# Attention part of a hybrid layer: softmax steps given priority, rotated blocks spread over the heads, weight halves moved from GpSimd to VectorE

## The chip, the cores and the metric

The kernel runs on one core of one Trainium2 chip. The metric is the device time of one execution in microseconds (us); lower is better. Times of whole runs are medians over several executions. The profile is one further execution recorded by the hardware profiler. PE is TensorE's matmul side, PEld its weight loads, DVE is VectorE, ACT is ScalarE, POOL is GpSimd, SP is SyncE, which issues most DMAs.

## The reference

One decoder layer on 1040 tokens (16 meta tokens and 1024 of input) of width 1024, in float32. A big projection gives the operands of two parallel branches: a retention with 4 heads and a differential attention with 8 heads. Both are merged by gates, and a gated MLP with a short convolution follows. The change touches the projections and the attention:

```
proj = u_pad @ w_in
rq, rk, rv, rg, dq, dk, dv, gates = split(proj)
rq = rope(rq); rk = rope(rk) * RET_DK ** -0.5
dq = rope(rmsnorm(dq, q_norm_w)); dk = rope(rmsnorm(dk, k_norm_w))
s = einsum('bhcqd,bhckd->bhcqk', dq_block, dk) * scale
p = softmax(where(mask, s, NEG))
a = p[:, :, 0] - lam * p[:, :, 1]
o = einsum('bhqk,bhke->bhqe', a, dv)
```

## The kernel before, in words

Float32 products are made of three fp32r matmuls: every operand is split into a high part and a low part (the rest), and high x high, high x low and low x high are summed in PSUM. For a weight block of 1024 x 128 this split is `split_half` (L226), called twice from `load_w` (L231): ACT casts half a block from `wr` into `wh` (L228), and POOL subtracts it from `wr` to give `wl` (L229), 128 x 512 elements each. `next_w` (L212) keeps two blocks loaded ahead.

`phase1` makes the projections and the 8 attention heads together. `projections` (L609) is a generator that works through a list of 128-column blocks, `seq`; each block is three accumulations of 24 matmuls into the two `acc` banks, and `evacuate` (L532) takes each one out of PSUM. What it costs depends on the kind. An `rv`, `rg`, `gd` or `gr` block costs one DVE multiply for each accumulation (L606). A `dk` or `dq` block costs ACT squares, a shuffle (L570) and multiplies on DVE (L571, L573) and POOL (L572). The rotary blocks `rk` and `rq` come in pairs: the first of a pair is only copied by ACT (L543); at the second, DVE makes two products from PSUM (L550, L551) and two more steps (L554, L555), and POOL makes two steps (L552, L553). L554 overwrites the buffer `x1` that L552 reads, so DVE waits there for POOL.

`attention(h)` (L661) is the other generator: eight blocks of 128 queries. For each block, `scores` makes the two score matrices on PE; DVE adds the mask and takes the row minimum (the scores carry a minus sign) (L686, L692); ACT makes the exponentials with row sums (L693); DVE inverts the sums (L697, L698); ACT scales the second matrix (L699); DVE combines both (L700). Then `turn` (L704) transposes the result on PE (L709), ACT and DVE split it (`ah`, `al`, L241 and L246), and PE multiplies it with the values into `ot`. Two query blocks are turned together, so each head has four groups of turns; in the first the second block has 272 columns, in the others 528, 784 and 1040. `prepare` (L622) splits keys and queries of the next head (L636, L637) and stacks them by DMAs from POOL's queue.

`blend` (L162) interleaves both generators: each attention step carries a weight, and 58 units of the projections, six to a block, are spread over a head. The instructions so recorded are then put in order by the framework's scheduler: each has a priority by its place in the program, and a model of the engines decides at what time which one goes first. Each engine then executes its own list in that order. PE's list follows the program nearly everywhere.

The list `seq` puts between the three blocks of each head's attention (dk, dq, dv) seven others. Before the change those are four `rv` blocks, then all 16 rotary blocks, then the remaining `rv` and `rg` blocks and the gates. So the rotary blocks fall into heads 0 to 2.

Of the kernel before, what the change touches and what calls it, by code (L numbers as in the profile page):

```python
# [13 lines left out]
AF = mybir.ActivationFunctionType  # L14
ALU = mybir.AluOpType
AX = mybir.AxisListType
# [12 lines left out]
RH, DH = 4, 8  # L29
# [68 lines left out]
class Builder:  # L98
    ATT_WEIGHT, RET_WEIGHT = 38.666666666666664, 27.0

    def __init__(self, ctx, tc, a, chunk_dec):
        self.tc, self.nc, self.a = tc, tc.nc, a
        self.chunk_dec = chunk_dec
        nc = self.nc
        self.V, self.A, self.G, self.E, self.S = nc.vector, nc.scalar, nc.gpsimd, nc.tensor, nc.sync
        pool = lambda n, b=1, **k: ctx.enter_context(tc.tile_pool(name=n, bufs=b, **k))
        self.cp = pool("cst")
        self.bp = pool("big", 34)
        self.wp = pool("w", 2)
        self.tp = pool("tmp", 2)  # L110
        self.ps = pool("ps", 2, space=PSUM)
        self.dr = pool("dr", 1, space=DRAM)
        self.n = 0
        self.later = []
        self.rot = 0

# [114 lines left out]
    def load_w(self, blk):  # L231
        w = self.tile_w()
        for i in (0, 4):
            self.split_half(w, self.raw_half(blk, i), i)
        return w

    def split(self, dh, dl, src, eh="A", el="V", scale=None):
# [423 lines left out]
    def attention(self, h):  # L661
        V, A, G, E, S = self.V, self.A, self.G, self.E, self.S
# [7 lines left out]
        def scores(t0, m, n, pieces):  # L670

            sm = self.tmp("sm", n=16, bufs=4)
            s = []
            for c in range(2):
                sc_ = self.big() if m > 2 else self.tmp("hs", n=16)
                for i, (a0, sz) in enumerate(pieces):
                    ps = self.sc()
                    self.mm(ps[:m, :sz], QA[c][:, t0:t0 + m], K[c][:, a0:a0 + sz], True, False)
                    self.mm(ps[:m, :sz], QB[c][:, t0:t0 + m], K[c][:, a0:a0 + sz], False, True)
                    if m == 2:  # L680
                        mk = self.hm[:m, :sz]
                    elif i == len(pieces) - 1:
                        mk = self.mask[:, 584 - sz:584]
                    else:
                        mk = self.mask[:, :sz]
                    V.tensor_tensor_reduce(out=sc_[:m, a0:a0 + sz], in0=ps[:m, :sz], in1=mk, scale=1.0, scalar=3e38,  # L686
                                           op0=ALU.add, op1=ALU.min, accum_out=sm[:m, 4 * c + i:4 * c + i + 1])
                np_ = len(pieces)
                mx = sm[:m, 4 * c:4 * c + 1]
                if np_ > 1:  # L690
                    mx = sm[:m, 4 * c + 3:4 * c + 4]
                    V.tensor_reduce(out=mx, in_=sm[:m, 4 * c:4 * c + np_], axis=AX.X, op=ALU.min)  # L692
                A.activation(sc_[:m, :n], sc_[:m, :n], AF.Exp, bias=mx, scale=-1.0,  # L693
                             accum_out=sm[:m, 10 + c:11 + c])
                s.append(sc_)
                yield 0.2 + n / 1000
            V.reciprocal(sm[:m, 12:14], sm[:m, 10:12])  # L697
            V.tensor_mul(sm[:m, 13:14], sm[:m, 13:14], self.nlam[:m])  # L698
            A.activation(s[1][:m, :n], s[1][:m, :n], AF.Copy, scale=sm[:m, 13:14])  # L699
            V.scalar_tensor_tensor(out=s[0][:m, :n], in0=s[0][:m, :n], scalar=sm[:m, 12:13], in1=s[1][:m, :n],  # L700
                                   op0=ALU.mult, op1=ALU.add)
            return s[0]

        def turn(pieces, meta=None):  # L704
# [18 lines left out]
        def rows(c):  # L723
            n = NMETA + P * (c + 1)
            k = -(-n // 512)
            sz = [2 * (n // (2 * k))] * k
            sz[0] += n - sum(sz)
            return (yield from scores(NMETA + P * c, P, n, [(sum(sz[:i]), sz[i]) for i in range(k)]))
# [3 lines left out]
        self.spill["do", h] = d, db  # L732
        outs = [(14, 258), (272, 256), (528, 256), (784, 256)]
        halo = yield from scores(HALO, 2, NMETA, [(0, NMETA)])
        ahead = yield from rows(0)

# [4 lines left out]
        for b in range(2):  # L741
            ps = self.tr()
# [5 lines left out]
        ps = self.tr()  # L748
# [4 lines left out]
        for p in range(4):  # L753
# [31 lines left out]
            for jj in range(p + 1):  # L785
# [4 lines left out]
                for kk in range(2):  # L790
                    j = 2 * jj + kk
                    lo = 128 if last and kk == 1 else 0
                    out = ot[:, o0 + lo:nq]
# [6 lines left out]
            t0, n = outs[p]  # L800
# [16 lines left out]
    def phase1(self):  # L817
        a = self.a
        self.spill = {}
        off = dict(rq=0, rk=8, rv=16, rg=32, dq=48, dk=56, dv=64, gr=72, gd=80)  # L820
        item = lambda k, i: (k, i, off[k] + i)
        dtiles = lambda h: [item("dk", h), item("dq", h), item("dv", h)]
        fill = []
        for h in range(RH):
            fill += [item("rk", 2 * h), item("rk", 2 * h + 1), item("rq", 2 * h), item("rq", 2 * h + 1)]
        for h in range(RH):
            fill += [item("rv", 4 * h + e) for e in range(4)] + [item("rg", 4 * h + e) for e in range(4)]
        fill = fill[16:20] + fill[:16] + fill[20:]
        fill += [item("gd", i) for i in range(8)] + [item("gr", i) for i in range(8)]
        seq = dtiles(0)  # L830
        for h in range(DH):
            f = fill[7 * h:7 * h + 7]
            dt = dtiles(h + 1) if h + 1 < DH else []
            seq += f[:3] + dt[:2] + f[3:4] + dt[2:] + f[4:]
        seq += fill[7 * DH:]
        order = []
        for n in range(0, NF, 2):
            down = [a["w_down"][n - 2], a["w_down"][n - 1]] if n else []
            up = [a["w_up"][f] for f in (n, NF + n, n + 1, NF + n + 1)]
            order += up[:2] + down + up[2:] if n < NF - 2 else up + down  # L840
        order += [a["w_down"][NF - 2], a["w_down"][NF - 1]]
        self.loaded = []
        self.stream = ([a["w_in"][b] for _, _, b in seq] + [a["w_ret_o"][i] for i in range(16)]
                       + [a["w_diff_o"][i] for i in range(8)] + [a["w_out"][i] for i in range(8)] + order)
        with self.tc.manual_schedule():
            self.norm_in()
            gen = self.projections(seq[2:])
            units = 6 * (len(seq) - 2)
            for _ in range(15):
                next(gen)  # L850
                units -= 1
        for _ in self.prepare(0):
            next(gen)
            units -= 1
        for _ in range(5):
            next(gen)
            units -= 1
        for h in range(DH):
            n = 58
            self.blend(self.attention(h), self.ATT_WEIGHT, gen, n)  # L860
            units -= n
        return gen, units


# [442 lines left out]
```

## Time and profile before

| | |
|---|---|
| median of 3 runs | 2567.45 us (2563.02 to 2570.38) |
| the profiled execution's own time | 2568.86 us |
| its span, first to last instruction | 2567.1 us |
| mean granted clock of TensorE | 0.993 |
| PE busy | 2509.6 us, 98% |
| DVE busy | 1550.9 us, 60% |
| ACT busy | 904.0 us, 35% |
| POOL busy | 816.8 us, 32% |
| the 8 heads, from the first score of head 0 to the end of head 7 | 108.5 to 1239 us of the span |

How to read it: matmuls overlap each other, so a busy PE can still be slower than it might be; what counts is the time in which PE or PEld stood idle, and what ended that wait. A head's window below runs from its first score matmul to that of the next head.

### The profile page before, as it was taken

To read this page: it belongs to the slowest core of one execution; us is meant where nothing else is said; L and a number is where in the kernel's file an instruction comes from. 1 tells how busy PE (TensorE), PEld (TensorE's weight loads), DVE (VectorE), ACT (ScalarE), POOL (GpSimd) and SP (SyncE) were. 2 spreads that over 40 slices of the span, in tenths; PEclk is the share of its full clock that TensorE was granted. 3 is DMA by queue.
4 is the path that set the end of the run, shared out by engine and by line. 5 is a ranking of instruction groups with operands and counts; after the bars stand their busy time and mean duration, and the time that the engine had idled before them with its cause. 6 is when DMAs were issued, how large, how long until landed. Compare 5 with 4: busy or idle time off the path is not lost. (4 is left out here: it accounts for less than half of the span.)

```text
span 2567.1 us, 40420 instructions
## 1 busy us (share of the span) xinstructions
PE 2509.6 (98%) x15444; PEld 2416.9 (94%) x15444; DVE 1550.9 (60%) x3228; ACT 904.0 (35%) x1881; POOL 816.8 (32%) x649
## 2 busy tenths in 40 slices
PE   8999999999999999999999999999999999999999
PEld 8899998999999999999998899999999999999998
DVE  7665757556463737453787887652555566555555
ACT  5343444444343525333466553332311111111111
POOL 1424343322222222222333332434332333333232
PEclk9999999999999999999999999999999999999999
DMA  4524242323324242423443434522111111111112
GB/s 165 129 84 108 63 115 71 107 76 93 104 81 120 62 121 65 117 84 104 116 107 90 105 99 134 185 93 99 38 50 46 50 50 41 50 50 42 50 50 87
DMA packets 171538, 224.55 MB, mean 87 GB/s; under 512 B 26712, under 2 KB 109264, under 8 KB 171344
## 3 DMA queue, kind: packets, MB, share of 16 engines
q1 hardware_dynamic: 165440, 202.70, 26.1%
q0 software_dynamic: 5760, 19.17, 3.5%
q8 instruction: 121, 1.98, 0.3%
q14 instruction: 73, 0.60, 0.1%
q10 hardware_dynamic: 144, 0.10, 0.0%
HBM read 160.20 MB, written 42.35 MB: 79 GB/s over the span
## 5 line engine op out<-in xcount | busy, mean ns | idle before, releaser
L175 PE MATMUL acc<-b,wh 128*128 128x342 f32 (+3 forms) x5948 | 1451.0, 326 | 15.7 <-DVE b L429 9.2
L175 PEld LDWEIGHTS acc<-b,wh 128*128 128x128 f32 x5948 | 1033.7, 190 | 28.4 <-issue 9.2
L175 PE MATMUL acc<-b,wl 128*128 128x342 f32 (+3 forms) x2974 | 966.9, 325 | 1.5 <-POOL wl L229 1.5
L229 POOL TENSOR_TENSOR wl<-wr,wh 128x512 fp32r<-128x512 f32 x366 | 507.6, 1404 | 1148.8 <-ACT wh L228 1136.5
L175 PE MATMUL sc<-b,wh 128*128 128x342 f32 (+2 forms) x2580 | 648.6, 334 | 1.1 <-ACT b L241 1.1
L175 PEld LDWEIGHTS acc<-b,wl 128*128 128x128 f32 x2974 | 564.1, 190 | 7.7 <-POOL wl L229 2.6
L175 PEld LDWEIGHTS sc<-b,wh 128*128 128x128 f32 x2580 | 455.2, 189 | 22.5 <-ACT b L241 1.3
L175 PE MATMUL sc<-b,wl 128*128 128x342 f32 (+2 forms) x1290 | 429.3, 334 | 0.0
L228 ACT CAST wh<-wr 128x512 fp32r<-128x512 f32 x366 | 212.8, 618 | 574.9 <-issue 241.2
L175 PEld LDWEIGHTS sc<-b,wl 128*128 128x128 f32 x1290 | 243.8, 189 | 10.0
L246 POOL TENSOR_TENSOR b<-b,b 128x512 fp32r<-128x512 f32 (+1 forms) x86 | 138.3, 1608 | 304.9 <-ACT b L241 262.7
L606 DVE TENSOR_TENSOR ev<-acc,b 128x342 f32<-128x342 f32 (+1 forms) x144 | 74.0, 514 | 187.7 <-PE acc L175 184.1
L241 ACT CAST b<-b 128x512 fp32r<-128x512 f32 (+3 forms) x137 | 102.1, 750 | 214.0 <-DVE b L1242 145.6
L693 ACT ACTIVATE b<-b,sm 128x272 f32<-128x272 f32 (+7 forms) x128 | 101.0, 789 | 150.4 <-DVE sm L692 118.6
L1205 DVE SCALAR_TENSOR_TENSOR b<-b,cols,b 128x1024 f32<-128x1024 f32 x88 | 148.8, 1691 | 2.3
L686 DVE CUSTOM_DVE_ANT_0 b<-sc,consts 128x144 f32<-128x144 f32 (+6 forms) x224 | 106.6, 503 | 39.3 <-PE sc L175 38.6
L1196 DVE TENSOR_TENSOR b<-sc,b 128x342 f32<-128x342 f32 x84 | 42.5, 511 | 139.4 <-PE sc L175 139.4
L246 DVE TENSOR_TENSOR al<-sc,ah 128x512 fp32r<-128x512 f32 (+2 forms) x144 | 77.6, 539 | 68.3 <-ACT ah L241 68.0
L241 ACT CAST ah<-sc 128x512 fp32r<-128x512 f32 (+2 forms) x144 | 67.3, 467 | 121.8 <-PE sc L709 84.0
L1220 DVE TENSOR_TENSOR b<-b,sc 128x512 f32<-128x512 f32 x117 | 78.7, 683 | 48.8 <-PE sc L175 48.8
L175 PE MATMUL sc<-b,b 128*128 128x264 f32 (+9 forms) x480 | 96.8, 319 | 1.9 <-DVE sm L686 1.9
L1203 DVE TENSOR_SCALAR b<-b,cols 128x1024 f32<-128x1024 f32 x44 | 81.5, 1853 | 1.6
(248 smaller groups left out, 2665.4 us busy)
## 6 DMA issues: line engine op xcount, KB each, us to landing
wr<-w_in SPq DMA_DIRECT2D x170, 256.0 KB
wr<-w_up SPq DMA_DIRECT2D x88, 256.0 KB
d<-ev SPq DMA_DIRECT2D x120, 171.0 KB
b<-b POOLq DMA_DIRECT2D x72, 260.0 KB, 4.6
b<-d SPq DMA_DIRECT2D x256, 64.0 KB
b<-d SPq DMA_DIRECT2D x24, 513.0 KB
wr<-w_down SPq DMA_DIRECT2D x44, 256.0 KB
b<-d SPq DMA_DIRECT2D x32, 260.0 KB
```

Source lines behind the costliest of these rows:

```text
L175: self.E.matmul(out, lhsT=l, rhs=r, start=start, stop=stop)
L228: self.A.copy(h, raw)
L229: (self.G if el == "G" else self.V).tensor_sub(l, raw, h.bitcast(F32))
L241: self.A.copy(dh, src)
L246: (self.V if el == "V" else self.G).tensor_sub(dl, src, dh.bitcast(F32))
L606: V.tensor_mul(o[:, :n], ps[:, :n], self.rb[:, cs])
L686: V.tensor_tensor_reduce(out=sc_[:m, a0:a0 + sz], in0=ps[:m, :sz], in1=mk, scale=1.0, scalar=3e38, op0=ALU.add, op1=ALU.min, accum_out=sm[ ...
L693: A.activation(sc_[:m, :n], sc_[:m, :n], AF.Exp, bias=mx, scale=-1.0, accum_out=sm[:m, 10 + c:11 + c])
L1196: self.V.tensor_mul(up[:, t0:t0 + n], ps[:, :n], self.rb2[:, t0:t0 + n])
L1203: V.tensor_scalar(out=o[:, q], in0=up[:, q], scalar1=self.cw(2, fi), scalar2=self.cb(fi), op0=ALU.mult, op1=ALU.add)
L1205: V.scalar_tensor_tensor(out=o[:, q], in0=up[:, NMETA - 2 + i:T - 2 + i], scalar=self.cw(i, fi), in1=o[:, q], op0=ALU.mult, op1=ALU.add)
L1220: self.V.tensor_add(h, h, ps)
```

## The change

Four edits, all in `phase1` and what it calls.

1. `load_w` takes the engine of the low part from `self.low`. It is "V" (DVE) while the loop over the 8 heads runs and "G" (POOL) otherwise.
2. The softmax instructions on DVE and ACT (L686 to L700 of before) are recorded with `high_priority(offset=300)`: the scheduler treats them as if they stood 300 places earlier.
3. The seven filler blocks of a head become five light ones and one pair of rotary blocks, in place of 16 rotary blocks in a row.
4. The order of the light blocks follows (rv and rg of each retention head, then gd, then gr).

```
+        self.low = "G"
...
-            self.split_half(w, self.raw_half(blk, i), i)
+            self.split_half(w, self.raw_half(blk, i), i, self.low)
...
-                    V.tensor_tensor_reduce(out=sc_[:m, a0:a0 + sz], in0=ps[:m, :sz], in1=mk, scale=1.0, scalar=3e38,
-                                           op0=ALU.add, op1=ALU.min, accum_out=sm[:m, 4 * c + i:4 * c + i + 1])
+                    with self.tc.high_priority(offset=300):
+                        V.tensor_tensor_reduce(out=sc_[:m, a0:a0 + sz], in0=ps[:m, :sz], in1=mk, scale=1.0, scalar=3e38,
+                                               op0=ALU.add, op1=ALU.min, accum_out=sm[:m, 4 * c + i:4 * c + i + 1])
...
+            with self.tc.high_priority(offset=300):
+                V.reciprocal(sm[:m, 12:14], sm[:m, 10:12])
+                V.tensor_mul(sm[:m, 13:14], sm[:m, 13:14], self.nlam[:m])
+                A.activation(s[1][:m, :n], s[1][:m, :n], AF.Copy, scale=sm[:m, 13:14])
+                V.scalar_tensor_tensor(out=s[0][:m, :n], in0=s[0][:m, :n], scalar=sm[:m, 12:13], in1=s[1][:m, :n],
+                                       op0=ALU.mult, op1=ALU.add)
...
+        light = [item(k, 4 * h + e) for h in range(RH) for k in ("rv", "rg") for e in range(4)]
+        light += [item("gd", i) for i in range(8)] + [item("gr", i) for i in range(8)]
+        pairs = [[item(k, 2 * h), item(k, 2 * h + 1)] for h in range(RH) for k in ("rk", "rq")]
         fill = []
...
-        fill = fill[16:20] + fill[:16] + fill[20:]
-        fill += [item("gd", i) for i in range(8)] + [item("gr", i) for i in range(8)]
+        for h in range(DH):
+            fill += light[5 * h:5 * h + 5] + pairs[h]
+        fill += light[5 * DH:]
...
+        self.low = "V"
         for h in range(DH):
             n = 58
             self.blend(self.attention(h), self.ATT_WEIGHT, gen, n)
             units -= n
+        self.low = "G"
```

The instruction lists of both programs have the same length on PE (15066 rows) and ACT (1648). DVE has 154 instructions more and POOL 154 fewer: the `wl` subtractions of 77 blocks. In the changed program line numbers are shifted: L686, L697, L698, L700 of before are L688, L701, L702, L704; L229 is L230, L246 is L247, L570 to L573 are L571 to L574, L552 and L553 are L553 and L554.

First place, POOL in head 0, where the first rotary pair is evacuated (`ev` and `sh` are rotary buffers, `wl` the low half of a weight block). Before:

```order
L552 TENSOR_TENSOR ev_1791<-x_1636,b_127 128x346
L553 TENSOR_TENSOR ev_1791<-ev_1791,sh_1793 128x346
L229 TENSOR_TENSOR wl_1860<-wr_1861,wh_1859 128x512
L552 TENSOR_TENSOR ev_1831<-x_1674,b_127 128x346
L229 TENSOR_TENSOR wl_1860<-wr_1865,wh_1859 128x512
L553 TENSOR_TENSOR ev_1831<-ev_1831,sh_1833 128x346
```

The same place after the change:

```order
L553 TENSOR_TENSOR ev_1932<-x_1784,b_127 128x346
L554 TENSOR_TENSOR ev_1932<-ev_1932,sh_1934 128x346
L644 DMA b_2149<-b_2037 64x1040
L553 TENSOR_TENSOR ev_1999<-x_1815,b_127 128x346
L554 TENSOR_TENSOR ev_1999<-ev_1999,sh_2001 128x346
```

No weight half stands between the rotary steps any more. In the DVE list the steps of a rotary pair now stand behind the L704 of 912 or of 1040 columns in heads 0 to 6, the last two softmaxes of a head, and behind those of 784 and 912 in head 7.

Second place, DVE in head 1, before the first group of turns (the softmax of 272 columns; `sql` and the `b_2695` rows belong to the evacuation of a dk or dq block). Before:

```order
L573 TENSOR_TENSOR b_2695<-b_2695,sh_2702 128x348
L264 TENSOR_TENSOR vm<-sc_2717,vm 16x128
L686 ISA b_2736,sm_2735<-sc_2737,consts 128x272
L686 ISA sm_2735 128x1
L686 ISA b_2768,sm_2735<-sc_2769,consts 128x272
L686 ISA sm_2735 128x1
L570 STREAM_SHUFFLE sh_2760<-b_2695 128x346
L246 TENSOR_TENSOR sql_2756<-sq_2754,sqh_2755 128x346
L571 TENSOR_TENSOR b_2695<-b_2695,b_125 128x346
L697 RECIPROCAL sm_2735<-sm_2735 128x2
L573 TENSOR_TENSOR b_2695<-b_2695,sh_2760 128x346
L698 TENSOR_TENSOR sm_2735<-sm_2735,nl 128x1
```

After:

```order
L688 ISA b_2694,sm_2693<-sc_2695,consts 128x272
L688 ISA sm_2693 128x1
L265 TENSOR_TENSOR vm<-sc_2675,vm 16x128
L688 ISA b_2726,sm_2693<-sc_2727,consts 128x272
L688 ISA sm_2693 128x1
L571 STREAM_SHUFFLE sh_2718<-b_2653 128x346
L247 TENSOR_TENSOR sql_2714<-sq_2712,sqh_2713 128x346
L701 RECIPROCAL sm_2693<-sm_2693 128x2
L572 TENSOR_TENSOR b_2653<-b_2653,b_125 128x346
L702 TENSOR_TENSOR sm_2693<-sm_2693,nl 128x1
L574 TENSOR_TENSOR b_2653<-b_2653,sh_2718 128x346
```

Of the softmax, the reciprocal and the multiply by lambda have moved up by one instruction each; the rest of the neighbourhood is the same.

Third place, DVE in head 1 before the second group of turns (528 columns), after the change; before it, nothing stood between L697, L698 and L700 here.

```order
L701 RECIPROCAL sm_2908<-sm_2908 128x2
L695 TENSOR_REDUCE sm_2963<-sm_2963 128x1
L230 TENSOR_TENSOR wl_2976<-wr_2977,wh_2975 128x512
L702 TENSOR_TENSOR sm_2908<-sm_2908,nl 128x1
L230 TENSOR_TENSOR wl_2976<-wr_2981,wh_2975 128x512
L594 TENSOR_TENSOR b_2480<-b_2480,b_2905 128x1040
L704 SCALAR_TENSOR_TENSOR b_2909<-b_2909,sm_2908,b_2933 128x528
```

Two weight halves and a normalisation (L594) now stand ahead of the combining step. Over all 64 softmaxes 30 of the 154 weight halves stand between a softmax's last minimum (L688) and its L704.

## Rows read from the trace of the kernel before

**Rows 1.** The page, busy time of each engine.

```profile
PE 2509.6 (98%) x15444; PEld 2416.9 (94%) x15444; DVE 1550.9 (60%) x3228; ACT 904.0 (35%) x1881; POOL 816.8 (32%) x649
```

**Rows 2.** Busy time by stretch, one for each head; columns PE, PEld, DVE, ACT, POOL, clock, DMA.

```profile
108.50:257.00 148.50, 140.15 (x894) 137.99 (x893) 90.53 (x214) 58.74 (x135) 53.68 (x52) 0.98 0.32 88
257.00:398.00 141.00, 137.65 (x894) 135.67 (x893) 91.44 (x212) 60.11 (x139) 54.05 (x52) 0.99 0.31 89
398.00:545.70 147.70, 140.47 (x896) 138.27 (x895) 87.56 (x214) 59.80 (x134) 48.21 (x46) 0.97 0.32 94
545.70:684.40 138.70, 136.17 (x896) 134.59 (x895) 79.06 (x199) 57.16 (x130) 37.29 (x35) 1.00 0.34 93
684.40:821.90 137.50, 136.18 (x896) 134.71 (x895) 76.69 (x199) 56.69 (x130) 37.05 (x35) 1.00 0.33 94
821.90:960.40 138.50, 136.49 (x896) 134.83 (x895) 76.41 (x199) 56.88 (x130) 36.20 (x34) 1.00 0.32 90
960.40:1101.50 141.10, 138.02 (x896) 135.85 (x895) 81.39 (x199) 55.78 (x128) 38.07 (x35) 0.99 0.33 92
1101.50:1239.00 137.50, 137.12 (x918) 135.81 (x918) 58.34 (x171) 55.04 (x121) 30.51 (x23) 1.00 0.32 95
```

**Rows 3.** Waits of PEld in the heads: total us, times, longest us.

```profile
PEld sc L709 <- DVE b L700: 23.4, 17, 3.5
PEld ot L175 <- DVE al L246: 4.4, 4, 2.0
PEld st L175 <- DVE sql L246: 3.1, 2, 2.7
PEld sc L175 <- DVE sm L686: 2.6, 2, 1.6
```

**Rows 4.** Order of time in head 0: start, us, engine, idle before and its releaser.

```profile
185.68 0.79 POOL L552 TENSOR_TENSOR ev<-x,b 128x346 f32<-128x346 f32 x1
186.43 1.26 POOL L229 TENSOR_TENSOR wl<-wr,wh 128x512 fp32r<-128x512 f32 x1
186.50 1.57 DVE L554 TENSOR_TENSOR x<-x,b 128x346 f32<-128x346 f32 x1 [1.09 <-POOL ev L552]
187.99 0.68 DVE L246 TENSOR_TENSOR al<-sc,ah 128x512 fp32r<-128x512 f32 x1
188.72 0.19 PEld L175 LDWEIGHTS ot<-al,vh 128*128 128x128 f32 x1 [1.91 <-DVE al L246]
```

**Rows 5.** Line L554 in the heads, duration min/median/max in ns.

```profile
L554 DVE TENSOR_TENSOR x<-x,b x24: 503/1112/1740, 175.2 to 492.4; 128x342 f32<-128x342 f32 x12, 128x346 f32<-128x346 f32 x8, 128x348 f32<-128x348 f32 x4
```

**Rows 6.** Waits in 100 to 1150 us: DVE for POOL.

```profile
DVE x L554 <- POOL ev L552: 13.2, 8, 3.4
```

**Rows 7.** Order of time in head 1, before the first group of turns.

```profile
270.94 0.44 DVE L686 CUSTOM_DVE_ANT_0 b<-sc,consts 128x272 f32<-128x272 f32 x1
273.73 1.25 DVE L571 TENSOR_TENSOR b<-b,b 128x346 f32<-128x346 f32 x1
275.08 0.52 DVE L573 TENSOR_TENSOR b<-b,sh 128x346 f32<-128x346 f32 x1
276.88 0.09 PEld L709 LDWEIGHTS sc<-consts,b 128*16 128x16 f32 x1 [2.65 <-DVE b L700]
```

**Rows 8.** The same place in head 5.

```profile
833.89 0.44 DVE L686 CUSTOM_DVE_ANT_0 b<-sc,consts 128x272 f32<-128x272 f32 x1 [1.72 <-PE sc L175]
838.61 0.09 PEld L709 LDWEIGHTS sc<-consts,b 128*16 128x16 f32 x1 [0.50 <-DVE b L700]
```

**Rows 9.** Line L229, duration min/median/max in ns on both engines.

```profile
L229 POOL TENSOR_TENSOR wl<-wr,wh x366: 1261/1294/2310, 39.6 to 2543.0; 128x512 fp32r<-128x512 f32 x183
L229 DVE TENSOR_TENSOR wl<-b,wh x4: 683/684/694, 10.4 to 15.1; 128x512 fp32r<-128x512 f32 x4
```

**Rows 10.** Line L571 in the heads, duration min/median/max in ns.

```profile
L571 DVE TENSOR_TENSOR b<-b,b x40: 508/1248/1269, 108.9 to 1006.8; 128x346 f32<-128x346 f32 x27, 128x348 f32<-128x348 f32 x13
```

**Rows 11.** Line L229 by head: the sum over the eight stretches.

```profile
sum 1130.50, DVE 0.00 POOL 211.93; mean DVE 0.00 POOL 26.49
```

More of the change, by code (lines that the diff above doesn't have):

```diff
@@ L685, in scores @@
                         mk = self.mask[:, :sz]
-                    V.tensor_tensor_reduce(out=sc_[:m, a0:a0 + sz], in0=ps[:m, :sz], in1=mk, scale=1.0, scalar=3e38,
-                                           op0=ALU.add, op1=ALU.min, accum_out=sm[:m, 4 * c + i:4 * c + i + 1])
+                    with self.tc.high_priority(offset=300):
+                        V.tensor_tensor_reduce(out=sc_[:m, a0:a0 + sz], in0=ps[:m, :sz], in1=mk, scale=1.0, scalar=3e38,
+                                               op0=ALU.add, op1=ALU.min, accum_out=sm[:m, 4 * c + i:4 * c + i + 1])
                 np_ = len(pieces)
[L689 to L694, printed above, removed]
+                with self.tc.high_priority(offset=300):
+                    mx = sm[:m, 4 * c:4 * c + 1]
+                    if np_ > 1:
+                        mx = sm[:m, 4 * c + 3:4 * c + 4]
+                        V.tensor_reduce(out=mx, in_=sm[:m, 4 * c:4 * c + np_], axis=AX.X, op=ALU.min)
+                    A.activation(sc_[:m, :n], sc_[:m, :n], AF.Exp, bias=mx, scale=-1.0,
+                                 accum_out=sm[:m, 10 + c:11 + c])
                 s.append(sc_)
                 yield 0.2 + n / 1000
[L697 to L701, printed above, removed]
+            with self.tc.high_priority(offset=300):
+                V.reciprocal(sm[:m, 12:14], sm[:m, 10:12])
[3 more added lines that the diff above has]
+                                       op0=ALU.mult, op1=ALU.add)
             return s[0]
@@ L822, in phase1 @@
         dtiles = lambda h: [item("dk", h), item("dq", h), item("dv", h)]
+        light = [item(k, 4 * h + e) for h in range(RH) for k in ("rv", "rg") for e in range(4)]
+        light += [item("gd", i) for i in range(8)] + [item("gr", i) for i in range(8)]
+        pairs = [[item(k, 2 * h), item(k, 2 * h + 1)] for h in range(RH) for k in ("rk", "rq")]
         fill = []
[L824 to L827, printed above, removed]
-        fill = fill[16:20] + fill[:16] + fill[20:]
-        fill += [item("gd", i) for i in range(8)] + [item("gr", i) for i in range(8)]
+        for h in range(DH):
+            fill += light[5 * h:5 * h + 5] + pairs[h]
+        fill += light[5 * DH:]
         seq = dtiles(0)
```

## The prediction

> **What bounds the kernel now.** I read the page's busy times first: PE is busy 98% of the span [rows 1], so whatever the change wins must come out of the rest, and only in the stretch that it touches. Next I read the busy time by stretch, with one stretch for each head [rows 2]. All heads hold the same matmuls (894 to 896, only the last has 918), yet they take 148.5, 141.0, 147.7, 138.7, 137.5, 138.5, 141.1 and 137.5 us, 1130.5 in all. Heads 0 to 2 are the slow ones, together 437.2 us against 414.7 for heads 3 to 5. They are also the heads with the rotary blocks: all 24 of the L554 steps lie between 175 and 492 us [rows 5]. DVE is busy about 90 us in them and 77 in heads 3 to 5, POOL 52 against 37. The granted clock is 0.97 to 0.99 of the 2.4 GHz level there and 1.00 in heads 3 to 5: short drops to 1.2 GHz follow the long waits, and cost about 148.5 x 0.02 + 141.0 x 0.01 + 147.7 x 0.03 = 8.8 us in three heads.
>
> Then the waits of PEld [rows 3]: 23.4 us in 17 waits for L700, the end of a softmax, before the transposes; 4.4 for the low part of the turned block, 3.1 for a low part of squares, 2.6 for a row minimum. That is 33.5 us, all for DVE, and with the drops of the clock it is what can be won, some 42 us.
>
> Last I read two places in order of time. In head 0 [rows 4] PE waits 1.91 us for the low part `al`. DVE was late with it because the rotary step L554 stood idle 1.09 us for POOL's L552, and then took 1.57 us while POOL ran a weight half. L554 takes 0.503 us at best and 1.112 at the median [rows 5], and DVE's waits there sum to 13.2 us in 8 times [rows 6]. In head 1 [rows 7] PE waits 2.65 us for the first group of turns; in head 5 the same instructions end in a wait of 0.50 us [rows 8]. The difference is the start: in head 5 DVE was idle for 1.72 us before its L686, in head 1 L686 follows a queue of rotary and dk steps.
>
> **The change, part by part.**
>
> *Weight halves leave POOL.* 154 subtractions go. On POOL one takes 1.294 us at the median, 26.5 us a head [rows 9, 11]; on DVE four of this size at the start took 0.684 us [rows 9], so DVE gets 154 x 0.684 = 105 us, 13 us a head. What POOL's halves cost DVE is given back in part. L571 shows the mechanism: beside its partner on POOL it takes 1.248 us, alone 0.508 [rows 10]. For L554 the excess over the best is 24 x (1.112 - 0.503) = 14.6 us, and 13.2 us of waiting come on top. Both were caused by a half on POOL in the place that I followed; I cannot say so of all 24. The DVE load of a head becomes 77 + 13 + one pair (heads 0 to 2 hold (90.5 + 91.4 + 87.6) - 3 x 77.4 = 37 us for 8 pairs, so 4.7), less a few: about 92 us of 138. That is as full as heads 0 and 1 are now, but with other contents; hence the first rival below.
>
> *Rotary blocks are spread.* One pair in each head, behind the softmax of 912 or 1040 columns in seven of eight. The backlog that entered the first turns of heads 1 and 2 came from rotary blocks behind the preceding head's last turn groups, three or more accumulations in a row; now one pair does that at most, without halves on POOL between its steps. Its price in a head is between nothing (it lies in DVE's idle 46 us) and (437.2 - 414.7) / 8 = 2.8 us (the whole excess of heads 0 to 2, shared by 8 pairs). I take nothing, because the excess in the places followed is POOL's queue and the backlog, not the steps themselves.
>
> *Softmax with priority.* The order shows what it does: L697 and L698 move up by one instruction, and L686 by one or two. At the first turns L698 passes L573 (0.52 us [rows 7]) and L697 passes L571, which does not shorten the chain. At most 0.5 us in each of the six heads that wait there, 3 us; it is small.
>
> *Halves on DVE.* A half waits for ACT's cast, and everything behind it on DVE waits too. 30 of 154 stand inside a softmax ahead of the combining step, 11 of them in the four softmaxes of a head that are turned first (272, 528 and 784 columns). Bounds: zero, if all fall into DVE's idle time; 30 x 0.684 = 20.5 us, if each delays PE in full. I take 4 us: half of the 11 exposed, since PE waited in 17 of 32 groups of turns.
>
> **The sum.** Heads 1 to 6 come to the level of heads 3 to 5, 138.2 us. Head 0 keeps its opening, where everything is loaded and the first turns find no softmax made ahead: 142. Head 7 stays at 137.5. 142 + 6 x 138.2 + 137.5 = 1108.7, which is 21.8 us less than 1130.5. Less 4 for halves on DVE: 17.8. The rest of the program (2567.1 - 1130.5 = 1436.6 us) holds the same work in the same order, and I give it nothing. The profiled execution took 2568.9 us, 1.4 above the median of the runs, so 2551.1 by its own time; 2551 is the forecast.
>
> **The rivals.**
>
> *The cost moves with the blocks: no change.* DVE will be as full in every head as in heads 0 and 1. If the load as such makes PE wait, every head takes what head 1 takes, 141.0: 1128, a gain of 2.5 us, so 2566. For it: the heads' times go with DVE's busy time. Against it: heads 0 and 1 have the same load and differ by 7.5 us, so places matter more than load. The change then also doesn't do what its priority says, since the order moves so little.
>
> *Halves block the queue: slower.* All 30 halves inside a softmax are exposed, 20.5 us, and the waits they make drop the clock in the five heads where it was 1.00 or nearly so, 3 us each as in head 0 (148.5 x 0.02): 35.5 - 21.8 = 13.7 us slower, 2583. It decides from 43 exposed halves, or 30 and the clock: (21.8 + 7.7) / 0.684. For it: two halves and a normalisation stand before L704 in the second group of head 1. Against it: DVE is idle a third of a head, and ACT's scaling step leaves a hole there anyway.
>
> In the rows, one DVE step that waited (L554, 1.09 us) held the `al` split behind it until PE stood 1.91 us [rows 4]. The Trainium skill, page TensorE: Matmul & The Clock Gate, section "Architectural detail", states that the queues of ScalarE and VectorE are strictly first in, first out. By that rule a half whose cast is late holds every softmax step behind it, and the sum would be this rival's 2583; by the row, PE feels only what arrives later than its own queue lasts, and the sum stays 2551. The trace agrees with the rule for L554; no row shows it for a half on DVE inside a head.
>
> *All heads like the best: larger gain.* 137.5 in each, 1100 in all, 30.5 less: 2538. It needs the waits at the first turns gone as well.
>
> **How the numbers follow.** Forecast 0.57, cost moves 0.19, slower 0.12, larger gain 0.12. A measurement of this kernel can tell about 0.3%, 7.7 us, from no change. The forecast's case with its unknown prices runs from 2543 to 2563, and a tenth of it lies within 0.3% of no change. So faster is 0.52 + 0.12 = 0.64, same 0.05 + 0.18 = 0.23, slower 0.12 + 0.01 = 0.13. The range takes in the larger gain and the case of no change and leaves out the slower one: 2536 to 2571.
>
> **What would show it.** Right: the eight stretches come out between 137 and 142 us with a clock of 0.99 or 1.00; PEld's waits for L700's successor fall from 23.4 us to 12 or less; DVE's wait of L554 for L552 nearly disappears; DVE is busy about 92 us in each head, POOL about 15 to 20. Wrong: heads 3 to 6 longer than 141, with waits for a combining step that stands behind a weight half; or PE waiting for a weight half itself, or for an evacuation of `acc` that DVE did too late.

## The result: 28 us less, and the profile after

The changed kernel takes 2539.83 us (median of 4 runs, 2539.29 to 2541.03) against 2567.59 in the same comparison: 0.9894 of the time before, 95% interval [0.9877, 0.9911]. The forecast was 2551, in a range of 2536 to 2571. So the sign held and the time lies in the range, but the gain is 27.8 us where the sum had 17.8, and one of its terms was far off. The time is nearest to the rival with all heads like the best, 2538, which had a chance of 0.12. Of all executions behind this document one, of r_only below, ran at a granted clock of 0.753 and took 3017.84 us; it is left out of that row.

The page of the changed kernel, busy time, and the group of the halves that moved:

```profile
PE 2497.5 (98%) x15444; PEld 2407.4 (95%) x15444; DVE 1597.8 (63%) x3382; ACT 908.0 (36%) x1883; POOL 607.6 (24%) x495
...
L230 DVE TENSOR_TENSOR wl<-wr,wh 128x512 fp32r<-128x512 f32 x154 | 107.3, 714 | 22.1 <-ACT wh L229 22.0
```

DVE took over 107 us of halves, yet is busy only 47 us longer than in [rows 1]; POOL lost 209 us. Busy time by stretch, one for each head, with the columns of [rows 2]:

```profile
108.90:246.30 137.40, 135.78 (x894) 134.34 (x894) 86.34 (x222) 56.48 (x129) 17.29 (x23) 1.00 0.34 95
246.30:383.40 137.10, 135.92 (x894) 134.39 (x893) 86.25 (x222) 56.62 (x130) 16.52 (x20) 1.00 0.33 96
383.40:523.40 140.00, 138.03 (x896) 136.30 (x895) 88.94 (x225) 57.19 (x130) 16.34 (x21) 0.99 0.31 89
523.40:663.10 139.70, 136.08 (x896) 134.61 (x895) 87.68 (x224) 57.13 (x131) 15.98 (x21) 1.00 0.35 92
663.10:801.20 138.10, 136.72 (x896) 135.10 (x895) 88.73 (x225) 58.52 (x133) 17.19 (x21) 1.00 0.34 94
801.20:937.20 136.00, 135.87 (x896) 134.40 (x895) 87.58 (x225) 58.16 (x133) 16.28 (x21) 1.00 0.32 91
937.20:1073.20 136.00, 135.65 (x896) 134.49 (x895) 87.70 (x224) 57.30 (x131) 16.48 (x21) 1.00 0.35 95
1073.20:1211.20 138.00, 137.16 (x918) 135.61 (x917) 72.12 (x197) 62.86 (x131) 10.56 (x9) 1.00 0.35 101
sum 1102.30, PE 1091.21 PEld 1079.23 DVE 685.34 ACT 464.26 POOL 126.63; mean PE 136.40 PEld 134.90 DVE 85.67 ACT 58.03 POOL 15.83
```

The heads take 1102.3 us, 28.2 less; the spans differ by 2567.1 - 2537.6 = 29.5. So the gain lies where the change is. Heads 0 to 2 gave 22.7 of it. The waits of PEld there, to be held against [rows 3]:

```profile
PEld sc L713 <- DVE b L704: 9.0, 10, 1.9
PEld ot L176 <- DVE al L247: 5.8, 5, 2.1
PEld sc L176 <- DVE sm L688: 0.7, 3, 0.3
```

The wait for the combining step fell from 23.4 to 9.0 us and the one for squares is gone; the one for `al` did not fall. All waits of PEld in the heads together fell from 37.2 to 17.3 us. By the traces' clock rows TensorE ran at 1.2 GHz for 23.9 us of the heads before, in six stretches, and for 3.4 us in the change, in one. If half of such time is lost (an estimate from the two clock levels), that is 10.2 us more. So the gain in the heads is about two parts waits and one part clock.

### The profile page after: what moved, and what is told of

Read it like the earlier page. It is cut to its first block, busy times and chain, and to the rows that moved or that the text cites. A ratio compares the mean times of both kernels' runs of the same rounds, so it can differ in the third digit from the quotient of the medians.

```text
span 2537.6 us, 40442 instructions
## 1 busy us (share of the span) xinstructions
PE 2497.5 (98%) x15444; PEld 2407.4 (95%) x15444; DVE 1597.8 (63%) x3382; ACT 908.0 (36%) x1883; POOL 607.6 (24%) x495
## 5 line engine op out<-in xcount | busy, mean ns | idle before, releaser
L230 POOL TENSOR_TENSOR wl<-wr,wh 128x512 fp32r<-128x512 f32 x212 | 297.4, 1423 | 608.6 <-ACT wh L229 608.4
L229 ACT CAST wh<-wr 128x512 fp32r<-128x512 f32 x366 | 213.0, 619 | 594.4 <-PE acc L176 249.8
L247 POOL TENSOR_TENSOR b<-b,b 128x512 fp32r<-128x512 f32 (+1 forms) x86 | 137.8, 1602 | 342.4 <-ACT b L242 317.1
L688 DVE CUSTOM_DVE_ANT_0 b<-sc,consts 128x144 f32<-128x144 f32 (+6 forms) x224 | 105.9, 504 | 41.0 <-PE sc L176 40.0
L573 POOL TENSOR_TENSOR sh<-sh,b 128x346 f32<-128x346 f32 (+1 forms) x42 | 43.1, 1026 | 358.7 <-DVE sh L571 358.7
L230 DVE TENSOR_TENSOR wl<-wr,wh 128x512 fp32r<-128x512 f32 x154 | 107.3, 714 | 22.1 <-ACT wh L229 22.0
L247 DVE TENSOR_TENSOR al<-sc,ah 128x512 fp32r<-128x512 f32 (+2 forms) x144 | 77.4, 538 | 43.2 <-ACT ah L242 42.1
```

The lines of the kernel that those rows point to most:

```text
L229: self.A.copy(h, raw)
L230: (self.G if el == "G" else self.V).tensor_sub(l, raw, h.bitcast(F32))
L247: (self.V if el == "V" else self.G).tensor_sub(dl, src, dh.bitcast(F32))
L573: G.tensor_mul(sh[:, :n], sh[:, :n], self.Sn[:, cs])
```

## The experiments: one part at a time

The parts of the change are independent: priority (P), spread of the rotary blocks (R), low halves on DVE (L). The edits are pieces of the diff above; each run leaves in the parts that it is named for and takes the others back, by these lines:

```
P  with self.tc.high_priority(offset=300):      # three places in scores
R  fill += light[5 * h:5 * h + 5] + pairs[h]     # else the order of before
L  self.low = "V"                                # else "G" throughout
```

Each run is compared with the kernel before measured beside it (2566.9 to 2567.9 us). P and R without L was not run.

| run | what it has | us | ratio, 95% interval |
|---|---|---|---|
| r_only | R | 2564.12 | 0.9987 [0.9978, 0.9996] |
| p_only | P | 2547.82 | 0.9924 [0.9911, 0.9938] |
| l_only | L | 2546.05 | 0.9916 [0.9903, 0.9930] |
| rl | R and L | 2545.94 | 0.9919 [0.9906, 0.9933] |
| the change | P, R and L | 2539.83 | 0.9894 [0.9877, 0.9911] |
| pl | P and L | 2530.21 | 0.9854 [0.9839, 0.9870] |

The theories of the first four runs were: A, GpSimd's halves stood between the rotary steps; B, the priority wins; C, the spread wins.

**L alone.**

> Weight halves on VectorE alone; rotary blocks in a row in heads 0 to 2 and softmax without priority, as before. Theory A (GpSimd's halves stood between the rotary steps and VectorE waited there): heads 0 to 2 fall from 437 us to about 422, heads 3 to 6 stay; 2553 in all, and the waits of the x1 step for GpSimd fall from 13.2 us to under 5. Theory B (the priority is what wins): 2565 or slower, since VectorE gets 105 us more without any order kept for the softmax. Theory C (the spread is what wins): 2563 to 2570.

Measured: 20.8 us gained, 7 us more than theory A had. Heads 0 to 2 take 424.5 us together, but heads 3 to 6, which were to stay, lose 7.5 us too, and 7.6 us of DVE's waits for POOL are left, not under 5. Theories B and C fall for this part.

**R alone.**

> Rotary pairs spread over the heads alone; halves on GpSimd, no priority. Theory A: the steps of each pair still stand behind halves on GpSimd, so each head has part of the price; heads 0 to 2 gain 14 us, heads 3 to 7 lose 5; 2559. Theory B: no change, 2566. Theory C (the backlog from rows of rotary blocks is what costs): heads 0 to 2 come to 138 to 140 and the others stay, 2548.

Measured: 2.7 us gained. Theory C falls. Busy time by stretch of this run, heads 0 and 3 and the sum:

```profile
106.84:247.25 140.41, 137.19 (x894) 135.82 (x893) 83.23 (x203) 56.33 (x129) 42.05 (x40) 0.99 0.33 93
...
531.13:675.40 144.27, 138.14 (x896) 136.17 (x895) 85.14 (x205) 56.81 (x131) 42.88 (x41) 0.99 0.33 90
...
sum 1129.14, PE 1102.19 PEld 1087.02 DVE 647.33 ACT 462.76 POOL 333.07; mean PE 137.77 PEld 135.88 DVE 80.92 ACT 57.84 POOL 41.63
```

Head 0 falls from 148.5 to 140.4 and head 3 rises from 138.7 to 144.3; the sum stays within 1.4 us of 1130.5. Heads 0 to 2 gain 12.9 us, near theory A's 14, but heads 3 to 7 lose some 12 where it had 5. For this part the first rival was right: the cost moves with the blocks.

**P alone.**

> Priority of the softmax alone; halves on GpSimd, rotary blocks in a row. Theory A: the order moves by an instruction or two, 2563. Theory B (the priority is what wins): waits of PE for the end of a softmax fall from 23.4 us to under 10, 2548. Theory C: 2565.

Measured: 19.0 us gained, from the part that I had called small. That is theory B's time, but its sign came only in part: PE's waits for the end of a softmax fall to 14.9 us, not under 10.

**R and L.**

> Halves on VectorE and rotary pairs spread, no priority: the whole change but for edit 2. Theory A: 2543, 3 us above the whole change. Theory B: 2560, most of the gain is lost. Theory C: as A for the spread, 2545.

Measured: 20.9 us gained, as L alone; theory B's 2560 falls. The spread adds nothing to the halves.

**P and L, no spread.**

> Priority and halves on VectorE, the rotary blocks in a row as before. Theory D (the spread adds nothing, priority and halves overlap in what they win): 2540 us, like the full change (2539.8), heads 0 to 2 together at most 3 us more than in the full change. Theory E (the spread is needed once both others are there, since it then takes the last backlog out of heads 0 to 2): 2545 or more, with heads 0 to 2 longer than 415 us.

Measured: 2530.21 us, 37.7 gained. Both theories missed: this is 9.6 us faster than the full change, and the two intervals do not overlap. Priority and halves nearly add up (19.0 + 20.8 = 39.8), and the spread takes a part back.

### What the priority does

The two halves of it apart: on the row minimum L688 alone (p_head), and on all later steps alone (p_tail); `nopri()` is a context that does nothing.

```
-                with self.tc.high_priority(offset=300):
+                with nopri():
```

> Priority on the row minimum (L687/L688) alone, all else as before. Theory F (the priority wins by letting the row minimum pass older evacuation steps on VectorE; from the last score matmul to the row minimum it is then some 1.7 us for the softmaxes made ahead, as with the full priority, against 2.95 before): at least 15 of the 19 us, 2548 to 2552. Theory G (it wins by the later steps, the reciprocal, the multiply and the combine): at most 5 us, 2562 to 2567.

> Priority on the later softmax steps alone (second minimum, exponential, reciprocal, multiply, scale, combine), the row minimum as before. Theory F: at most 5 us gained, 2562 to 2567. Theory G: at least 15 us gained, 2548 to 2552.

Measured: p_head 2557.80 us (0.9963 [0.9950, 0.9975]), p_tail 2560.30 us (0.9971 [0.9961, 0.9982]): 10.1 and 7.6 us. Neither theory holds alone; the parts add up to 17.7 of 19.0. The traces show what the priority moves. DVE in order of time in head 5 of the kernel before, behind the first group of turns; the row minimum here belongs to the softmax of 400 columns, which is made ahead of its turn:

```profile
839.48 0.55 DVE L570 STREAM_SHUFFLE sh<-b 128x346 f32<-128x346 f32 x1
839.91 0.50 DVE L246 TENSOR_TENSOR sql<-sq,sqh 128x346 fp32r<-128x346 f32 x1
840.33 1.25 DVE L571 TENSOR_TENSOR b<-b,b 128x346 f32<-128x346 f32 x1
841.62 0.41 DVE L264 TENSOR_TENSOR am<-sc,am 16x258 fp32r<-16x258 f32 x1
842.07 0.52 DVE L573 TENSOR_TENSOR b<-b,sh 128x346 f32<-128x346 f32 x1
842.50 0.42 DVE L246 TENSOR_TENSOR al<-sc,ah 128x256 fp32r<-128x256 f32 x1
842.84 0.57 DVE L686 CUSTOM_DVE_ANT_0 b<-sc,consts 128x400 f32<-128x400 f32 x1
```

The same place with the priority alone (p_only):

```profile
826.42 0.55 DVE L571 STREAM_SHUFFLE sh<-b 128x346 f32<-128x346 f32 x1
826.86 0.55 DVE L688 CUSTOM_DVE_ANT_0 b<-sc,consts 128x400 f32<-128x400 f32 x1
...
827.34 1.02 DVE L247 TENSOR_TENSOR sql<-sq,sqh 128x346 fp32r<-128x346 f32 x1
828.28 0.51 DVE L572 TENSOR_TENSOR b<-b,b 128x346 f32<-128x346 f32 x1
828.71 0.15 DVE L701 RECIPROCAL sm<-sm 128x2 f32<-128x2 f32 x1
```

The row minimum passes five steps of an evacuation and a turn, and comes 2.9 us sooner after the shuffle. Over all 64 softmaxes, by the traces: mean us from the end of a softmax's own last score matmul to the end of its row minimum or of its combining step, for the 32 made ahead (144, 400, 656 and 912 columns) and the 32 turned next (272, 528, 784 and 1040); then, for the heads, all waits of PEld and the time at 1.2 GHz.

| run | row minimum, ahead | combined, ahead | combined, next | PEld waits | at 1.2 GHz |
|---|---|---|---|---|---|
| before | 2.95 | 6.51 | 6.55 | 37.2 | 23.9 |
| p_head | 1.85 | 6.54 | 6.77 | 32.7 | 6.8 |
| p_tail | 3.00 | 6.52 | 6.27 | 32.9 | 13.7 |
| p_only | 1.65 | 5.67 | 6.03 | 23.0 | 13.7 |

An early row minimum alone (p_head) does not bring the combined matrix earlier, and PE waits only 4.5 us less; much of what that profiled execution gains, the fastest of its five, is time at the lower clock. With both parts the combining step comes earlier for both kinds, and the waits fall by 14.2 us, where the parts alone take off 4.5 and 4.3. So theory F's mechanism, the row minimum passing older steps, is seen, but it is not what wins by itself. Why the clock fell less often in p_head was not followed.

### What the halves on GpSimd cost

l_only has its halves on DVE; l_dummy has them there too, and GpSimd then makes a subtraction of the same size in place on the raw buffer, of which nobody reads the result.

```
         (self.G if el == "G" else self.V).tensor_sub(l, raw, h.bitcast(F32))
+        if el == "V" and self.low == "V":
+            self.G.tensor_sub(raw, raw, h.bitcast(F32))
```

> The low parts are made on VectorE in the heads, as in the run with that part alone (2546.1), and GpSimd does a subtraction of the same size on the raw buffer in place afterwards, whose result nobody reads. Theory H (what the halves cost was GpSimd's presence: slower VectorE steps beside it and rotary steps that wait behind a half): the gain of 20.8 us falls to 5 or less, 2562 to 2572, and VectorE's L555 waits for GpSimd come back to 10 us or more in the heads. Theory I (the gain comes from the low parts being ready earlier or from the new order on VectorE): it stays, 2545 to 2551.

Measured: 2565.92 us, 0.9994 [0.9985, 1.0002]. The whole gain is gone, and theory H holds. The heads' sums, first l_only:

```profile
sum 1110.16, PE 1092.31 PEld 1078.92 DVE 694.08 ACT 460.59 POOL 123.32; mean PE 136.54 PEld 134.87 DVE 86.76 ACT 57.57 POOL 15.41
```

Then l_dummy, with its wait of DVE for POOL:

```profile
sum 1129.36, PE 1099.08 PEld 1084.15 DVE 738.43 ACT 459.99 POOL 353.36; mean PE 137.39 PEld 135.52 DVE 92.30 ACT 57.50 POOL 44.17
...
DVE x L557 <- POOL ev L555: 13.5, 15, 1.7
```

The same instructions of DVE take 44 us longer when POOL's subtractions run beside them, and DVE waits 13.5 us for POOL in place of 7.6. The other reading of this run is worth as much: l_dummy does all that the kernel before does and 154 halves on DVE besides, and its heads take 1129.4 us against 1130.5. By this comparison no price of the halves on DVE can be seen. It is a balance over eight heads, though: head 0 takes 153.0 us against 148.5, head 2 142.5 against 147.7.

**The wait, and one thing more.** In the kernel before, the rotary product goes into the PSUM bank instead of over `x1`, so that DVE need not wait for POOL there. With that the add behind it reads only one operand from SBUF.

```
-            V.tensor_mul(x1[:, :n], x1[:, :n], self.sinr[:, cs])
-            V.tensor_add(o2[:, :n], o2[:, :n], x1[:, :n])
+            V.tensor_mul(ps[:, :n], x1[:, :n], self.sinr[:, cs])
+            V.tensor_add(o2[:, :n], o2[:, :n], ps[:, :n])
```

> The kernel before with one edit: the product of the rotary copy with the sine goes into the PSUM bank instead of over x1 (L554, L555), so VectorE never waits there for GpSimd's L552; halves stay on GpSimd, no priority, no spread. Theory M (of what GpSimd's halves cost, the waits of VectorE for rotary steps behind them are the larger part): 10 to 16 us gained of the 20.8 that the halves alone gave, 2551 to 2557. Theory N (the larger part is that VectorE's steps run slower beside GpSimd's): 0 to 8 us, 2559 to 2567, with heads 0 to 2 still above 428 us together.

Measured: 2557.97 us, 0.9966 [0.9954, 0.9978]: 9.8 us, between the two theories. Heads 0 to 2 take 425.3 us together, below theory N's 428. The run cannot decide between the two, because the add became faster as well; its duration before (L555) and in this run (L556), min/median/max in ns:

```profile
L555 DVE TENSOR_TENSOR ev<-ev,x x24: 503/522/1746, 176.8 to 494.3; 128x342 f32<-128x342 f32 x12, 128x346 f32<-128x346 f32 x8, 128x348 f32<-128x348 f32 x4
...
L556 DVE TENSOR_TENSOR ev<-ev,acc x24: 493/506/516, 175.2 to 480.3; 128x342 f32<-128x342 f32 x12, 128x346 f32<-128x346 f32 x8, 128x348 f32<-128x348 f32 x4
```

Both rotary steps together take 33.9 us of DVE in place of 45.2, and PE waits 3.7 us for the bank that is now freed later. So 9.8 us is what the 13.2 us of waiting [rows 6] and some 11 us of slower steps cost together, less what the bank costs. Nor are the waits all the halves' doing. In the trace of before five of the eight (6.2 us) are for a POOL step that came straight behind a half, two (3.8 us) for one that itself waited for a spill transfer, and for the eighth (3.2 us) the profile names no cause; with the halves gone 7.6 us were left.

### What the spread costs

The changed kernel in order of time before one of its two longest waits for `al`, in head 2: first POOL, then DVE, then PEld, and as a last row DVE before the `al` of head 1:

```profile
484.52 0.79 POOL L553 TENSOR_TENSOR ev<-x,b 128x346 f32<-128x346 f32 x1 [3.67 <-DMA d<-ev]
...
485.34 0.52 DVE L555 TENSOR_TENSOR x<-x,b 128x346 f32<-128x346 f32 x1 [1.38 <-POOL ev L553]
485.90 1.28 DVE L556 TENSOR_TENSOR ev<-ev,x 128x346 f32<-128x346 f32 x1
487.10 0.50 DVE L607 TENSOR_TENSOR ev<-acc,b 128x342 f32<-128x342 f32 x1
487.52 1.27 DVE L247 TENSOR_TENSOR al<-sc,ah 128x512 fp32r<-128x512 f32 x2
...
488.25 0.19 PEld L176 LDWEIGHTS ot<-al,vh 128*128 128x128 f32 x1 [1.97 <-DVE al L247]
...
348.73 0.52 DVE L607 TENSOR_TENSOR ev<-acc,b 128x346 f32<-128x346 f32 x1 [3.70 <-DMA d<-ev]
```

The chain begins at a transfer: POOL's step waits for the spill of an earlier `ev` buffer to DRAM, DVE for POOL, the split of the turn behind DVE's step, and PE for the split. No half stands in it. In head 1 DVE itself stands 3.70 us for such a spill; in head 3 it stands 3.72 us for POOL, and what held POOL there the profile does not name. The wait for `al` comes five times with the spread and once in pl:

```profile
PEld ot L176 <- DVE al L247: 2.1, 1, 2.1
```

Three runs tried the two ways out: the product into PSUM, in the full change (af_x1) and without the spread (pl_x1), and priority for the split of the turn as well (pl_turn).

> The full change, but the product of the rotary copy with the sine goes into the PSUM bank instead of over x1 (L555, L556), so VectorE no longer waits there for GpSimd's L553. Theory J (what the spread costs beside priority and halves, some 10 us, is VectorE standing for a GpSimd step that waits for the spill transfer, just ahead of the split of a turn): 2530 to 2534, the waits of the value product for the low part al fall from 5.8 us to 2 or less. Theory K (the cost is the load of the rotary steps in heads that were light before): no more than 3 us gained, 2537 to 2542.

> Priority and halves on VectorE without the spread (2530.2), with the same product into PSUM. Theory J: the one long wait for al in head 0 (2.1 us and the clock drop behind it, some 4 us) goes, 2525 to 2528. Theory K: 2529 to 2532, and so little gained that the spread's price must lie elsewhere.

> Priority and halves on VectorE without the spread, and priority for the split of a turn (ah, al) as well. If the place of al in VectorE's list is what is late: 2525 to 2528. If it is late because its engine stands for another, or if the split now holds up the softmax steps: 2529 to 2536, with the waits for the combining step (9.8 us) grown.

Measured: af_x1 2533.64 us (0.9869 [0.9853, 0.9886]), pl_x1 2527.36 us (0.9848 [0.9833, 0.9863]), pl_turn 2529.48 us (0.9854 [0.9839, 0.9869]). The product into PSUM wins 6.2 us in the full change, and PE's wait for `al` falls from 5.8 to 0.8 us, with 2.2 us of a new wait for the bank:

```profile
PEld acc L176 <- DVE ev L556: 2.2, 3, 1.4
...
PEld ot L176 <- DVE al L247: 0.8, 1, 0.8
```

So that chain is shown, though the add became faster here too (12.1 us in all for 15.2). Without the spread it wins 2.9, which is not clear of the noise, and head 0 goes from 141.8 to 138.0. Priority for the split changes nothing that can be told (0.7 us), and the wait for the combining step does not grow (7.3 us). But af_x1 still lies 6.3 us behind pl_x1, so theory J accounts for some 3 of the 9.6 us. Of the rest only a part is in the heads. By the profiled executions the heads take 1102.3 us in the change and 1100.2 in pl, 1097.6 in af_x1 and 1094.6 in pl_x1: 2 to 3 us. The spread gives 4.4 us in head 0 and takes 6.6 in heads 1 to 3. The two profiled executions differ by only 5.8 us in their spans, since that of pl lies 3.4 us above its median. Much of what is left shows far behind them, in the MLP, where all programs hold the same matmuls. A stretch of 695 us from the same point of it, first in the changed kernel:

```profile
1794.50:2489.50 695.00, 694.82 (x3998) 656.53 (x3997) 413.52 (x439) 118.72 (x172) 227.54 (x143) 1.00 0.15 47
```

And in pl:

```profile
1793.00:2488.00 695.00, 694.80 (x4015) 655.74 (x4014) 417.39 (x442) 119.80 (x173) 229.95 (x145) 1.00 0.15 47
```

PE has no gap in either and the clock is at 2.4 GHz, yet one does 17 matmuls more, some 3 us; from the same matmul, the 4198th from the end, to the end of the span it is 744.9 against 740.6 us. The pair af_x1 and pl_x1, from one chip, shows the same (744.9 and 741.3). This goes with the program, and not with the spread alone: it is 744.7 to 745.2 us in the kernel before, the change, af_x1, x1_only, p_only, p_head and p_tail, 742.8 to 743.4 in r_only, l_only, rl and l_dummy, and 740.6 to 741.3 in pl, pl_x1 and pl_turn, whatever the chip. r_only has the spread and p_only has not. So the 9.6 us hold some 4 us, and the gains of r_only and l_only some 2 us, that no mechanism in the heads explains. What sets this pace was not found.

## Why the prediction came out as it did

**What bounds the kernel: right.** Nearly all of the gain came out of the heads, mostly 0 to 2, through PE's waits for DVE, and the granted clock rose with them. The signs that I had named came: stretches of 136 to 140 us, a wait for the combining step of 9.0 us (12 or less was named), POOL at 16 us a head. DVE is busy 86 to 89 us in heads 0 to 6, a little less than the 92 named. One failed: DVE's wait of L555 for L553, which was to nearly vanish [rows 6], is 11.9 us in 6 times.

```profile
DVE x L555 <- POOL ev L553: 11.9, 6, 3.7
```

**Halves leave POOL: the size was right, the steps behind it only in part.** The sum gave 21.8 us for halves and spread; L and R together gave 20.9, and L alone 20.8. But I read the excess of L554, the rotary product, as the work of the halves, from one place. In the trace of before only 8 of the 24 run beside a half. In l_only, with no half on POOL, its median is still 1.108 us (1.112 before [rows 5]):

```profile
L555 DVE TENSOR_TENSOR x<-x,b x24: 508/1108/1743, 173.7 to 479.4; 128x342 f32<-128x342 f32 x12, 128x346 f32<-128x346 f32 x8, 128x348 f32<-128x348 f32 x4
```

20 of the 24 there run beside POOL's own second rotary step. What the halves cost is spread over many steps of DVE, 44 us in all. The Trainium skill, page SBUF — State Buffer, section "Who interferes with whom", states that a VectorE instruction with two SBUF inputs contends with a GpSimd instruction that reads SBUF. The runs agree: 738.4 against 694.1 us for the same DVE instructions with and without POOL's subtractions.

**Softmax with priority, "at most 0.5 us in each of the six heads that wait there, 3 us; it is small": this step failed.** It gave 19.0 us alone, 16 on top of the halves (l_only to pl), and 6.1 in the full change (rl to the change; 6.9 if each is held against the kernel before measured beside it). I judged it by one place of the order, before the first turns, where the row minimum moves by one or two instructions. That softmax is the one turned next, and over all of that kind the row minimum does not gain: the mean from score to row minimum is 1.15 us before and 1.27 in p_only. The softmaxes made ahead gain 1.3 us each there, and with the later steps moved too the combining step of both kinds comes 0.5 to 0.8 us sooner. I counted the halves over all 64 softmaxes, but not what the priority moves.

**Rotary blocks spread, price nothing: too little.** Alone it gave 2.7 us, with the halves nothing, with both others it cost 9.6 by the medians. Of that 2 to 3 us are in the heads, as set out above, and about half has no cause that was found. I had argued that the excess of heads 0 to 2 was POOL's queue and the backlog. The chain from the spill transfer to `al` was in the trace of before too: at 214.89 us POOL's L552 starts after 4.4 us of waiting for a spill, DVE has stood 3.4 us for it, and PE then waits 2.0 us for `al`. I saw only the name of L552 and did not ask what it waited for.

**Halves on DVE, 4 us: none found.** By l_dummy the heads with DVE's halves are as long as those of before. DVE does stand for ACT's cast, 22.0 us in 16 times in the changed kernel (the last group of the page above), but PE feels none of it that could be seen. The slower rival, with halves that block the queue, had its wait but not its price.

**Head 0 at 142: 137.4.** With P and L alone it is 141.8, and 138.0 once the rotary product goes to PSUM: part of what I took for its opening was the rotary wait. Its opening wait is still there, at 1.9 us where it was 3.5.

Of the 10.0 us of gain that the sum missed (27.8 against 17.8), 6.9 are what the change gains beyond R and L (27.8 against 20.9), the priority less what the spread took back, and 3.1 what R and L gained beyond 17.8, about the charge for halves on DVE. That the forecast came as near as it did is in part luck: two larger errors, 16 us for the priority on top of the halves and 10 us for the spread beside both others, have opposite signs.

A version that beats both kernels is pl_x1, the change without the spread and with the product in PSUM: 2527.36 us, 12.5 less than the change and 40 less than before.

## What to carry to other kernels

Where an in-order engine serves several chains, judge a change of priorities over all its places, also those that are not late themselves, and over all steps of a chain: here moving its first step or its later ones alone took far less off PE's waits than moving both. When an engine waits for a helper engine, follow the wait one step further; here it ended at a transfer that freed a buffer. And take the parts of a change apart even when it wins: here the kernel without one of the three parts was 9.6 us faster.

## What the runs showed of the hardware

An instruction of 128 x 1 elements with two SBUF inputs, the multiply by lambda, takes 159 ns at the median and up to 1274 beside POOL in the kernel before:

```profile
L698 DVE TENSOR_TENSOR sm<-sm,nl x72: 146/159/1274, 112.3 to 1186.6; 128x1 f32<-128x1 f32 x64, 2x1 f32<-2x1 f32 x8
```

The seven that took over 163 ns, 537 to 1274, all ran beside an instruction of POOL. The step stands in every softmax between the row sums and ACT's scaling. The rotary add, by contrast, never took more than 516 ns once one of its operands came from PSUM (x1_only), where it had taken up to 1746.

And the pace of the same matmuls in a stage without gaps differs by 0.4% between programs, 3998 against 4015 in 695 us, while programs that share it agree across chips (743.1 and 743.4 us in l_only and l_dummy). That is as large as some of the parts measured here; a difference of a few us is to be looked for in its own stage before it is put down to an edit.
